# A hybrid decoder step on one NeuronCore: rows gathered three ahead, fewer of them beside the early second products, and six buffers for the spilled activations

## Chip, cores and metric

The kernel runs on one NeuronCore of one Trainium2 chip. The metric is the device time of one execution in microseconds (us), the median over runs.

## What is computed

One layer of a decoder for 512 prompt tokens and 64 sample tokens, all in float32: projections, a short convolution and a sliding-window attention, merged and normalised to `h`, and then a mixer that draws 16 experts for each of 8 heads of each token out of 16384 (128 x 128 keys):

```python
qv = jnp.einsum('nd,de->ne', xb, w_pq)                # queries
s = jnp.einsum('nhpc,hpkc->nhpk', qv, sub_keys)       # scores of the two halves of a key
top_s, top_i = lax.top_k(s, PEER_TOPK)                # 16 of each half, then 16 of their pairs
gate = jax.nn.softmax(best_s, axis=-1)
pre = jnp.einsum('nd,nhkd->nhk', xb, expert_u[idx])
coef = gate * jax.nn.gelu(pre)
out = jnp.einsum('nhk,nhkd->nd', coef, expert_v[idx])
y = _layer_norm(DEEPNORM_ALPHA * h + out, ln2_g, ln2_b)
```

## The kernel before

**Every product in three.** A weight tile of 128x1024 comes from HBM as `raw`. ScalarE rounds it to a high part `whi` and another engine subtracts to get the low part `wlo` (`split`, L118 to L120, called by `table`, L136). The TensorE takes each product as high by high, low by high and high by low (`mm3`, L122).

**Two ways to the experts.** The tokens are cut in five chunks. For three of them (`DENSE`, 384 token slots, `ND`) all 128 blocks of 128 experts are computed: a *first product* for block t (`front`, L856: the activations by `euT[t]`, 24 matmuls, then Gelu) and a *second product* (`back` and `accumulate`, L916 and L922: the Gelu values, weighted, by `ev`, 18 matmuls into six PSUM banks). Between them `middle` (L898) multiplies by the weights `gm` that say which token chose which expert, and splits the result in `chi` and `clo`. That multiplication and `clo` are VectorE's. For the other two chunks (192 columns of slots) the chosen rows alone are fetched: `experts` (L491) is a generator of 384 jobs, 192 rows of `eu` and then 192 of `ev`. GpSimd gathers a row tile `g` of 128x1024 by indirect DMA (L512), and VectorE multiplies it (`junk`, L526; `h`, L535). `GLAG = 2` rows are fetched ahead, in `GBUF = 4` buffers.

**The order of the work.** Rows are drawn by `side(n)`, which `table` calls with `pace` behind a weight's low part, on that low part's engine. In the stretch of the first products two rows and one row take turns (`PACE_U`). A weight of the scores takes none, a second product with t < NS = 60 takes one, a later one three (`PACE_V`). A scheduler puts each engine's instructions in an order when the program is built, and the engine keeps it.

**The stages.** First the projections and merges (until some 515 us). Then the scores of the dense chunks (16 weights `w_pq`), top 16 and `route` on VectorE, with 20 first products between them. Then `gate_matrix` (L774) builds one-hot tiles `hot` (`OB = 3` buffers) and writes the weights to HBM (`gd`), beside more first products. In all `AHEAD = NS + LAG = 69` first products are made by then. Those with t < 60 do not fit in SBUF: they go to HBM (`spill`) and `middle` reads them back into `re`, which has 3 buffers. Then come the *early second products*, t from 0 to 59, without first products beside them; the low part of their weight is VectorE's. `gm` is read for eight t at a time, in three DMAs. From t = 60 on each second product has a first product beside it, LAG = 9 ahead, until block 127's first product is done; the last nine second products are alone again. Then the rows end, and the three dense chunks and the rows' chunks are normalised (`finish`, L544).

Of the kernel before, what the change touches and what calls it, by code (L numbers as in the profile page):

```python
# [23 lines left out]
SEQ = 512  # L24
# [22 lines left out]
ND = 128 * len(DENSE)  # L47
# [3 lines left out]
NE = 128  # L51
NS = 60
LAG = 9
AHEAD = NS + LAG
GBUF = 4
GLAG = 2
RAW = dict(w=3, v=3)
HI = dict(w=4, v=2)
OB = 3

# [7 lines left out]
PACE_N = 18  # L68
PACE_A, PACE_B, PACE_U, PACE_V = (1, 0), (2, 1, 1), (2, 1), (1, 3)
LO_N = 50  # L70
# [5 lines left out]
def step_kernel(ctx: ExitStack, tc: tile.TileContext, I: dict, O: dict):  # L76
# [3 lines left out]
    pools = {}  # L80
# [23 lines left out]

    loads, newest = [], [None, None]

# [29 lines left out]
    def table(src, p, eng, pace=0):  # L136
        raw = tmp(p, [128, 1024], "raw", bufs=RAW[p])
        newest[0] = S.dma_start(raw, src).ins
        hi = tmp(p, [128, 1024], "whi", bufs=HI[p], dt=F32R)
        lo = tmp(p, [128, 1024], "wlo", bufs=HI[p], dt=F32R)  # L140
        last = split(hi, lo, raw, eng)
        if pace:
            with tc.issue_after(last.ins):
                side(pace)
        return hi, lo
# [16 lines left out]
    make_identity(nc, ident)  # L162
    mask_p = const("mask_p", [128, 256], src=I["mask_p"])
    convw = const("convw", [128, 4, 3], src=I["conv_w"])
# [7 lines left out]
    state = const("state", [128, 4, 8, 2], src=I["state"])  # L172
    kT_all = const("kT_all", [128, SEQ])
    v_all = const("v_all", [128, 5, 128])

# [405 lines left out]
    def weight(s, src):  # L581
        s.units += 1
        if s.w == 0:
            return table(src, "w", G if s.units % 3 != 1 else V)
        if s.units > LO_N:
            return table(src, "w", G)
        pace = PACE_A if s.units <= PACE_N else PACE_B
        if s.units % 4 == 3:
            return table(src, "w", V)
        return table(src, "w", G, pace[s.units % len(pace)])  # L590
# [219 lines left out]
    ks, bs = ExitStack(), ExitStack()  # L810
    pools["k"] = ks.enter_context(pool("k", "left"))
    pools["mm"] = ks.enter_context(psum("mm", 3))
    at_stack = ExitStack()
    pools["at"] = at_stack.enter_context(psum("at", 3))
# [26 lines left out]
    for k, tag in enumerate(("chi", "clo")):  # L841
        ln2.append(tmp("a", [128, D], tag, name=f"ln2{k}"))
        late(ln2[k], I["ln"][2 + k].broadcast_to([128, D]))
    at_stack.close()
    pools["at"] = ks.enter_context(psum("at1", 1))
# [5 lines left out]
    pools["f"] = ctx.enter_context(pool("f", "right"))  # L851
    pools["b"] = bs.enter_context(pool("b", "right"))
    hT = second.hT
# [24 lines left out]
    for k, g4 in enumerate((0, 2, 1, 3)):  # L878
        scores(second, g4)
        fronts(FQ * (k + 1))  # L880
    total = len(DENSE) * 128 // GN
    base = done
# [15 lines left out]
    def middle(t):  # L898
# [5 lines left out]
        if t < NS:  # L904
            ge = tmp("v", [128, ND], "re", bufs=3)
            S.dma_start(ge, spill[t])
        else:
            ge = coef[t]
# [7 lines left out]
    def back(t):  # L916
        co = coef.pop(t)
        wv = table(I["ev"][t * 128:(t + 1) * 128, :], "vw"[t < NS or t >= NE - LAST], V if t < NS or t > NE - 4 else G,
                   PACE_V[t >= NS])
        return co, wv  # L920

    def accumulate(ts, i, halves):  # L922
# [7 lines left out]
        return calls  # L930

    for t in range(NE + 1):
        fronts(t + LAG)
        if t < NE:
            middle(t)
        if 1 <= t <= NE - LAST:
            ops = [(t - 1, *back(t - 1))]
            for i in range(len(DENSE)):
                for args, kw in accumulate(ops, i, (0, 1)):
                    PE.matmul(*args, **kw)  # L940
# [111 lines left out]
```

## Time and profile before

| | us |
|---|---|
| median of 3 runs | 1854.08 (1852.5 to 1858.05) |
| the profiled execution | 1850.18 |
| span of its instructions | 1848.4 |
| TensorE busy with matmuls | 1723.9 (93%) |
| VectorE busy | 1464.7 (79%) |
| GpSimd busy | 1109.6 (60%) |
| ScalarE busy | 781.4 (42%) |

The span runs from the first instruction to the last, and 1.8 us lie around it. Busy shares are means over stages with different limits, so the trace is read stage by stage. In rows of the trace PE is TensorE, DVE is VectorE, ACT is ScalarE, POOL is GpSimd and SPq is the queue from which most DMAs are issued. In square brackets stands how long the engine was idle before an instruction and what ended that.

### The profile page before, as it was taken

How to read it: one execution, taken by the hardware profiler on the slowest of the kernel's cores; microseconds unless marked ns; L12 is line 12 of the kernel's file. 1: busy time of each engine (PE TensorE's matmuls, PEld its weight loads, DVE VectorE, ACT ScalarE, POOL GpSimd, SP SyncE). 2: the span in 40 equal slices, each digit the busy share in tenths (PEclk: the TensorE clock that was granted, in tenths of full speed). 3: DMA queues.
4: the chain of work that ended last, by engine and by line, in shares of the span. 5: the costliest groups of instructions: out<-in, count | busy, mean ns of one | idle time of the engine just before them, and what ended most of it. 6: DMA issues, size and time to landing. Idle time of an engine off the chain costs nothing.

```text
span 1848.4 us, 27569 instructions
## 1 busy us (share of the span) xinstructions
PE 1723.9 (93%) x9760; PEld 1566.4 (85%) x9760; DVE 1464.7 (79%) x2588; ACT 781.4 (42%) x1337; POOL 1109.6 (60%) x724
## 2 busy tenths in 40 slices
PE   7999998998799999899888899999999999999985
PEld 7998898988489899799878778778999999999974
DVE  5634579998965699987893778779788878888887
ACT  4554444443233344377794333333333333343322
POOL 4445434367857777798645422224678787778783
PEclk9999999999989999899999999999999999999998
DMA  7446443368757789899748899999999999989873
GB/s 252 134 150 225 138 132 122 115 200 300 249 201 241 235 294 311 271 349 348 289 188 303 317 333 335 336 346 339 333 314 345 337 324 350 353 307 343 314 268 104
DMA packets 190539, 496.50 MB, mean 269 GB/s; under 512 B 17712, under 2 KB 83696, under 8 KB 187312
## 3 DMA queue, kind: packets, MB, share of 16 engines
q1 hardware_dynamic: 135104, 293.39, 46.5%
q0 software_dynamic: 55296, 201.35, 30.2%
q8 instruction: 76, 1.25, 0.3%
q14 instruction: 63, 0.52, 0.1%
HBM read 454.48 MB, written 40.54 MB: 268 GB/s over the span
## 4 chain that ended last, share of the span: by engine, by line
PE 40%; DVE 23%; DMA 14%; issue 9%; POOL 8%; ACT 4%; SPq 1%; DVEq 0%; POOLq 0%; ACTq 0%
PE acc L940 15%; PE ps L123 7%; PE ps L124 7%; PE ps L125 7%; DMA g<-in_ev,idx 5%; POOL wlo L120 4%; POOL g L512 4%; DVE junk L526 3%; PE ps L796 3%; DMA re<-spill 2%; DVE wlo L120 2%; DMA raw<-in_ev 2%; DMA raw<-in_w_o 1%; ACT whi L119 1%; ACT hot L793 1%
## 5 line engine op out<-in xcount | busy, mean ns | idle before, releaser
L120 POOL TENSOR_TENSOR wlo<-raw,whi 128x1024 fp32r<-128x1024 f32 x232 | 579.1, 2499 | 301.8 <-ACT whi L119 264.7
L119 ACT ACTIVATE whi<-raw 128x1024 fp32r<-128x1024 f32 x388 | 409.5, 1056 | 603.9 <-PE ps L124 236.1
L123 PE MATMUL ps<-xhi,whi 128*128 128x384 f32 (+2 forms) x1600 | 529.9, 331 | 21.6 <-ACT sp L863 13.4
L125 PE MATMUL ps<-xhi,wlo 128*128 128x384 f32 (+2 forms) x1600 | 526.1, 329 | 3.5 <-POOL wlo L120 2.0
L124 PE MATMUL ps<-xlo,whi 128*128 128x384 f32 (+2 forms) x1600 | 526.1, 329 | 0.0
L535 DVE SCALAR_TENSOR_TENSOR h<-g,pre,h 128x1024 f32<-128x1024 f32 x192 | 309.8, 1614 | 68.3 <-DMA g<-in_ev,idx 66.8
L512 POOL DMA_INDIRECT g<-in_eu,idx x192 | 204.2, 1063 | 233.1 <-DVE junk L526 186.9
L123 PEld LDWEIGHTS ps<-xhi,whi 128*128 128x128 f32 x1600 | 308.4, 193 | 31.0 <-ACT sp L863 15.1
L512 POOL DMA_INDIRECT g<-in_ev,idx x192 | 257.0, 1338 | 124.9 <-DVE h L535 77.9
L125 PEld LDWEIGHTS ps<-xhi,wlo 128*128 128x128 f32 x1600 | 307.8, 192 | 5.3 <-POOL wlo L120 2.3
L124 PEld LDWEIGHTS ps<-xlo,whi 128*128 128x128 f32 x1600 | 308.3, 193 | 2.9 <-issue 0.3
L940 PE MATMUL acc<-whi,chi 128*128 128x512 f32 x756 | 291.4, 392 | 14.5 <-ACT chi L119 8.2
L940 PE MATMUL acc<-wlo,chi 128*128 128x512 f32 x756 | 296.9, 393 | 7.6 <-POOL wlo L120 7.6
L940 PE MATMUL acc<-whi,clo 128*128 128x512 f32 x756 | 256.4, 392 | 1.1 <-DVE clo L120 1.1
L120 DVE TENSOR_TENSOR wlo<-raw,whi 128x1024 fp32r<-128x1024 f32 x156 | 203.5, 1304 | 46.0 <-ACT whi L119 43.6
L940 PEld LDWEIGHTS acc<-whi,chi 128*128 128x128 f32 x756 | 142.6, 189 | 46.7 <-ACT chi L119 11.5
L940 PEld LDWEIGHTS acc<-wlo,chi 128*128 128x128 f32 x756 | 142.4, 188 | 38.0 <-POOL wlo L120 9.7
L526 DVE SCALAR_TENSOR_TENSOR junk<-g,hp 128x1024 bf16<-128x1024 f32 x104 | 125.9, 1210 | 56.8 <-DMA g<-in_eu,idx 54.8
L940 PEld LDWEIGHTS acc<-whi,clo 128*128 128x128 f32 x756 | 142.4, 188 | 31.3 <-DVE clo L120 1.6
L526 DVE SCALAR_TENSOR_TENSOR junk<-g,h 128x1024 bf16<-128x1024 f32 x88 | 130.9, 1488 | 3.3 <-DMA g<-in_eu,idx 3.0
L796 PE MATMUL ps<-hot 128*128 128x128 f32 x768 | 113.4, 290 | 14.5 <-ACT hot L793 13.4
L787 DVE TENSOR_TENSOR hot<-pt,T 128x1024 f32<-128x1024 f32 x96 | 113.9, 1218 | 15.8 <-PE ps L796 12.7
(250 smaller groups left out, 2157.9 us busy)
## 6 DMA issues: line engine op xcount, KB each, us to landing
raw<-in_euT SPq DMA_DIRECT2D x128, 512.0 KB
raw<-in_ev SPq DMA_DIRECT2D x128, 512.0 KB
gd<-gb SPq DMA_DIRECT2D x24, 1024.0 KB
gm<-gd SPq DMA_DIRECT2D x48, 512.0 KB
raw<-in_w_g SPq DMA_DIRECT2D x32, 512.0 KB
raw<-in_w_pq SPq DMA_DIRECT2D x32, 512.0 KB
raw<-in_w_bch SPq DMA_DIRECT2D x24, 512.0 KB
spill<-sp SPq DMA_DIRECT2D x60, 192.0 KB
```

The source lines that it names most:

```text
L119: A.activation(hi, src, AF.Copy)
L120: return (eng or V).tensor_tensor(lo, src, hi.bitcast(F32), op=ALU.subtract)
L123: PE.matmul(ps, L[0], R[0], start=start, stop=False)
L124: PE.matmul(ps, L[0], R[1], start=False, stop=False)
L125: PE.matmul(ps, L[1], R[0], start=False, stop=stop)
L512: G.indirect_dma_start(out=rows[i], out_offset=None, in_=I[src], in_offset=bass.IndirectOffsetOnAxis(ap=idx[c][:, s:s + 1], axis=0))
L526: V.scalar_tensor_tensor(junk, g, 1.0, in_psum(c), op0=ALU.mult, op1=ALU.mult, accum_out=p)
L535: V.scalar_tensor_tensor(h_tok[c], g, p, h_tok[c], op0=ALU.mult, op1=ALU.add)
L787: V.tensor_tensor(hot, iota_ps.unsqueeze(1).unsqueeze(1).broadcast_to([128, 2, 4, 128]), T[:, 0:2, n:n + 4].unsqueeze(3).broadcast_to([128 ...
L793: A.activation(oi, oi, AF.Copy, scale=weight_of)
L796: newest[1] = PE.matmul(ps[:, r * 128:(r + 1) * 128], hot[:, 1, r, :], oi, start=True, stop=True).ins
L940: PE.matmul(*args, **kw)
```

## The change

Nothing of the arithmetic changes. The edits:

- `GLAG` 2 to 3 and `GBUF` 4 to 5: rows are fetched three ahead, in five buffers.
- A weight of the dense chunks' scores now draws one row (`PACE_Q = 1`). Of three early second products two draw a row, where each did.
- `NS` 60 to 63 and `LAG` 9 to 6: AHEAD stays 69. Three more blocks are spilled and read back, three fewer are kept.
- `re` has 6 buffers, `hot` has 4.
- For t up to 63, what `middle(t)` puts on VectorE is ordered behind the low part of the weight of the second product two back (`last_lo`, in fact that of t - 2).
- To make room, the mask, `kT_all` and `v_all` of the attention lie in a pool that is closed after it, and the pool `b` is opened anew before the gates.

```diff
@@ -49,14 +49,14 @@
 NG = ND // GN
 IB = 8
 NE = 128
-NS = 60
-LAG = 9
+NS = 63
+LAG = 6
 AHEAD = NS + LAG
-GBUF = 4
-GLAG = 2
+GBUF = 5
+GLAG = 3
 RAW = dict(w=3, v=3)
 HI = dict(w=4, v=2)
-OB = 3
+OB = 4
 
 
 ORDER = "qkscscasacsca"
@@ -66,7 +66,7 @@
 
 
 PACE_N = 18
-PACE_A, PACE_B, PACE_U, PACE_V = (1, 0), (2, 1, 1), (2, 1), (1, 3)
+PACE_A, PACE_B, PACE_Q, PACE_U, PACE_V = (1, 0), (2, 1, 1), 1, (2, 1), (1, 3)
 LO_N = 50
 GATED = "aaag"
 OUT = "aaav"
@@ -102,7 +102,7 @@
     def tmp(p, shape, tag, name=None, bufs=1, dt=F32):
         return pools[p].tile(shape, dt, tag=tag, name=name or tag, bufs=bufs)
 
-    loads, newest = [], [None, None]
+    loads, newest = [], [None, None, None]
 
     def late(dst, src):
 
@@ -139,6 +139,7 @@
         hi = tmp(p, [128, 1024], "whi", bufs=HI[p], dt=F32R)
         lo = tmp(p, [128, 1024], "wlo", bufs=HI[p], dt=F32R)
         last = split(hi, lo, raw, eng)
+        newest[2] = last.ins
         if pace:
             with tc.issue_after(last.ins):
                 side(pace)
@@ -160,7 +161,6 @@
 
     ident = const("ident", [128, 128])
     make_identity(nc, ident)
-    mask_p = const("mask_p", [128, 256], src=I["mask_p"])
     convw = const("convw", [128, 4, 3], src=I["conv_w"])
     sink_p = const("sink_p", [128, 8], src=I["sink_p"])
     sink_s = const("sink_s", [128, 2, 2], src=I["sink_s"])
@@ -170,8 +170,6 @@
     ucar = const("ucar", [128, 4, 2])
     V.memset(ucar, 0.0)
     state = const("state", [128, 4, 8, 2], src=I["state"])
-    kT_all = const("kT_all", [128, SEQ])
-    v_all = const("v_all", [128, 5, 128])
 
     iota128 = const("iota128", [128, 128], src=I["iota128"])
     h_tok, idx, gate = {3: const("h3", [128, D])}, {}, {}
@@ -583,7 +581,7 @@
         if s.w == 0:
             return table(src, "w", G if s.units % 3 != 1 else V)
         if s.units > LO_N:
-            return table(src, "w", G)
+            return table(src, "w", G, PACE_Q)
         pace = PACE_A if s.units <= PACE_N else PACE_B
         if s.units % 4 == 3:
             return table(src, "w", V)
@@ -810,6 +808,11 @@
     ks, bs = ExitStack(), ExitStack()
     pools["k"] = ks.enter_context(pool("k", "left"))
     pools["mm"] = ks.enter_context(psum("mm", 3))
+    kvs = ExitStack()
+    pools["kv"] = kvs.enter_context(pool("kv", "right"))
+    mask_p, kT_all = tmp("kv", [128, 256], "mask_p"), tmp("kv", [128, SEQ], "kT_all")
+    v_all = tmp("kv", [128, 5, 128], "v_all")
+    loads.insert(0, (mask_p, I["mask_p"]))
     at_stack = ExitStack()
     pools["at"] = at_stack.enter_context(psum("at", 3))
     sel3 = ([tmp("k", [128, 128], f"k3{k}") for k in range(2)], tmp("k", [128, 128], "gt3"))
@@ -841,6 +844,7 @@
     for k, tag in enumerate(("chi", "clo")):
         ln2.append(tmp("a", [128, D], tag, name=f"ln2{k}"))
         late(ln2[k], I["ln"][2 + k].broadcast_to([128, D]))
+    kvs.close()
     at_stack.close()
     pools["at"] = ks.enter_context(psum("at1", 1))
     shared = [pools["at"].tile([128, 512], F32, tag="at", name="pt")]
@@ -849,7 +853,7 @@
     scratch.append(shared[0])
     pools["hp"] = ks.enter_context(psum("hp", 1))
     pools["f"] = ctx.enter_context(pool("f", "right"))
-    pools["b"] = bs.enter_context(pool("b", "right"))
+    pools["b"] = bs.enter_context(pool("b0", "right"))
     hT = second.hT
     coef = {}
 
@@ -878,6 +882,8 @@
     for k, g4 in enumerate((0, 2, 1, 3)):
         scores(second, g4)
         fronts(FQ * (k + 1))
+    bs.close()
+    pools["b"] = bs.enter_context(pool("b", "right"))
     total = len(DENSE) * 128 // GN
     base = done
     for i in range(len(DENSE)):
@@ -902,7 +908,7 @@
                 S.dma_start(gm[0][:, g:g + NG // 3].rearrange("p g i n -> p g (i n)"),
                             gd[g:g + NG // 3, :, t:t + IB, :].rearrange("g p i n -> p g (i n)"))
         if t < NS:
-            ge = tmp("v", [128, ND], "re", bufs=3)
+            ge = tmp("v", [128, ND], "re", bufs=6)
             S.dma_start(ge, spill[t])
         else:
             ge = coef[t]
@@ -916,7 +922,7 @@
     def back(t):
         co = coef.pop(t)
         wv = table(I["ev"][t * 128:(t + 1) * 128, :], "vw"[t < NS or t >= NE - LAST], V if t < NS or t > NE - 4 else G,
-                   PACE_V[t >= NS])
+                   PACE_V[1] if t >= NS else PACE_V[0] * (t % 3 > 0))
         return co, wv
 
     def accumulate(ts, i, halves):
@@ -929,12 +935,18 @@
                                   dict(start=(t == 0 and p == 0), stop=(t == NE - 1 and p == 2))))
         return calls
 
+    last_lo = None
     for t in range(NE + 1):
         fronts(t + LAG)
-        if t < NE:
+        if last_lo is not None and t <= NS:
+
+            with tc.issue_after(last_lo):
+                middle(t)
+        elif t < NE:
             middle(t)
         if 1 <= t <= NE - LAST:
             ops = [(t - 1, *back(t - 1))]
+            last_lo = newest[2] if t <= NS else None
             for i in range(len(DENSE)):
                 for args, kw in accumulate(ops, i, (0, 1)):
                     PE.matmul(*args, **kw)
```

Three places of the order. **GpSimd, in the dense chunks' scores** (`wlo<-raw,whi` is a weight's low part, `g<-in_eu` the gather of a row; before):

```order
L512 DMA g<-in_eu,idx_95 128x1024 x2
L120 TENSOR_TENSOR wlo<-raw,whi 128x1024 x5
L512 DMA g<-in_eu,idx_95 128x1024 x2
L120 TENSOR_TENSOR wlo<-raw,whi 128x1024
L512 DMA g<-in_eu,idx_95 128x1024
L120 TENSOR_TENSOR wlo<-raw,whi 128x1024
```

and with the change:

```order
L510 DMA g<-in_eu,idx_92 128x1024
L120 TENSOR_TENSOR wlo<-raw,whi 128x1024
L510 DMA g<-in_eu,idx_92 128x1024
L120 TENSOR_TENSOR wlo<-raw,whi 128x1024
L510 DMA g<-in_eu,idx_92 128x1024
L120 TENSOR_TENSOR wlo<-raw,whi 128x1024 x2
L510 DMA g<-in_eu,idx_92 128x1024 x2
```

The runs of five low parts, the score weights, have rows between them now.

**VectorE, where the second products begin** (`re<-re,gm` is the weighting in `middle`, `junk` a row; before):

```order
L910 TENSOR_TENSOR re<-re,gm 128x384 x2
L120 TENSOR_TENSOR clo<-re,chi 128x384 x2
L526 SCALAR_TENSOR_TENSOR junk,pre<-g,hp 128x1024
L910 TENSOR_TENSOR re<-re,gm 128x384
L526 SCALAR_TENSOR_TENSOR junk,pre<-g,hp 128x1024 x2
L910 TENSOR_TENSOR re<-re,gm 128x384 x2
L526 SCALAR_TENSOR_TENSOR junk,pre<-g,hp 128x1024
L120 TENSOR_TENSOR wlo<-raw,whi 128x1024
L526 SCALAR_TENSOR_TENSOR junk,pre<-g,hp 128x1024
L120 TENSOR_TENSOR wlo<-raw,whi 128x1024
```

and with the change:

```order
L916 TENSOR_TENSOR re<-re,gm 128x384 x2
L120 TENSOR_TENSOR clo<-re,chi 128x384 x2
L524 SCALAR_TENSOR_TENSOR junk,pre<-g,hp 128x1024 x4
L120 TENSOR_TENSOR wlo<-raw,whi 128x1024
L916 TENSOR_TENSOR re<-re,gm 128x384
L524 SCALAR_TENSOR_TENSOR junk,pre<-g,hp 128x1024 x2
L120 TENSOR_TENSOR wlo<-raw,whi 128x1024
L916 TENSOR_TENSOR re<-re,gm 128x384
```

Five weightings stood before the first low part, two do now.

**GpSimd, at the end** (the low parts of the last second products and the last gathers; before):

```order
L120 TENSOR_TENSOR wlo<-raw,whi 128x1024
L512 DMA g<-in_ev,idx_98 128x1024 x3
L120 TENSOR_TENSOR wlo<-raw,whi 128x1024
L512 DMA g<-in_ev,idx_98 128x1024
L120 TENSOR_TENSOR wlo<-raw,whi 128x1024
L512 DMA g<-in_ev,idx_98 128x1024 x3
L120 TENSOR_TENSOR wlo<-raw,whi 128x1024 x2
```

and with the change:

```order
L120 TENSOR_TENSOR wlo<-raw,whi 128x1024
L510 DMA g<-in_ev,idx_95 128x1024 x3
L120 TENSOR_TENSOR wlo<-raw,whi 128x1024
L510 DMA g<-in_ev,idx_95 128x1024 x3
L120 TENSOR_TENSOR wlo<-raw,whi 128x1024
L510 DMA g<-in_ev,idx_95 128x1024 x5
```

The last two low parts stood behind all gathers; now five gathers stand behind the last low part.

## Rows read from the trace of the kernel before

**Rows 1.** Busy time by stretch; columns as in the second line.

```profile
core 0 of [0], span 1848.4 us
core 0: us, PE busy (x) PEld busy (x) DVE busy (x) ACT busy (x) POOL busy (x), PEclk, DMA share, GB/s
516.00:640.00 124.00, 123.05 (x747) 118.18 (x745) 68.14 (x299) 46.11 (x68) 84.14 (x49) 0.99 0.70 235
640.00:780.00 140.00, 125.10 (x701) 122.55 (x702) 139.62 (x424) 56.41 (x78) 107.05 (x67) 0.95 0.83 283
780.00:901.00 121.00, 121.00 (x814) 120.80 (x813) 100.00 (x123) 86.91 (x209) 104.86 (x97) 0.99 0.95 346
901.00:978.00 77.00, 62.55 (x413) 55.31 (x412) 71.29 (x74) 68.36 (x198) 35.03 (x54) 0.96 0.52 209
978.00:1033.00 55.00, 45.12 (x247) 44.34 (x245) 22.23 (x23) 18.07 (x25) 30.30 (x18) 0.93 0.89 303
1033.00:1296.00 263.00, 254.46 (x1106) 208.61 (x1107) 210.36 (x313) 91.52 (x122) 74.90 (x66) 0.99 0.98 338
1296.00:1781.00 485.00, 485.00 (x2451) 441.28 (x2450) 412.65 (x353) 172.84 (x237) 375.08 (x229) 1.00 0.92 329
```

**Rows 2.** Chain that ended last: second products; start us, us, what.

```profile
1249.89 24.79 PE acc L940 x108
...
1470.16 4.12 PE acc L940 x18
...
1478.47 4.12 PE acc L940 x18
```

**Rows 3.** Waits of PE, 1033 to 1296 us: total, times, longest.

```profile
PE acc L940 <- ACT chi L119: 8.2, 8, 1.6
PE acc L940 <- ACT whi L119: 5.3, 1, 5.3
```

**Rows 4.** DMA, 1033 to 1296 us: all packets; the rows' queue (packets, MB, share).

```profile
DMA packets 50800, 88.94 MB, mean 338 GB/s; under 512 B 3244, under 2 KB 34834, under 8 KB 50782
...
q0 software_dynamic: 9293, 33.87, 34.9%
```

**Rows 5.** Timeline near 1140 us, by engine: start us, us, instruction, [idle before].

```profile
1129.84 4.94 SPq L902 DMA_DIRECT2D gm<-gd  x3
...
1137.90 0.85 SPq L906 DMA_DIRECT2D re<-spill  x2
...
1146.00 0.56 DVE L910 TENSOR_TENSOR re<-re,gm 128x384 f32<-128x384 f32 x1 [4.42 <-DMA re<-spill]
...
1147.22 0.50 PE L940 MATMUL acc<-whi,chi 128*128 128x512 f32 x1 [0.98 <-ACT chi L119]
```

**Rows 6.** Timeline, 1010 to 1034 us, PE and DVE.

```profile
1012.80 0.69 PE L123 MATMUL ps<-xhi,whi 128*128 128x384 f32 x1 [4.85 <-ACT gel L867]
...
1014.40 4.58 DVE L910 TENSOR_TENSOR re<-re,gm 128x384 f32<-128x384 f32 x2 [10.17 <-DMA re<-spill]
...
1021.16 3.42 DVE L120 TENSOR_TENSOR wlo<-raw,whi 128x1024 fp32r<-128x1024 f32 x1 [1.04 <-ACT whi L119]
```

**Rows 7.** Groups of DVE, 640 to 780 us: xcount | busy us, mean ns | idle before.

```profile
L526 DVE SCALAR_TENSOR_TENSOR junk<-g,hp 128x1024 bf16<-128x1024 f32 x35 | 42.1, 1203 | 0.0
```

**Rows 8.** Waits: DVE from 516 to 640 us, then PE from 640 to 783 us.

```profile
DVE junk L526 <- DMA g<-in_eu,idx: 52.8, 10, 14.3
...
PE ps L123 <- ACT sp L863: 12.9, 3, 6.3
```

**Rows 9.** Timeline of the end, DVE and POOL.

```profile
1771.77 1.22 DVE L120 TENSOR_TENSOR wlo<-raw,whi 128x1024 fp32r<-128x1024 f32 x1
...
1807.09 1.36 POOL L512 DMA_INDIRECT g<-in_ev,idx  x1 [0.30 <-issue]
...
1810.13 6.77 DVE L535 SCALAR_TENSOR_TENSOR h<-g,pre,h 128x1024 f32<-128x1024 f32 x3 [2.02 <-DMA g<-in_ev,idx]
```

**Rows 10.** Waits of PE, 1781 to 1831 us.

```profile
PE acc L940 <- POOL wlo L120: 7.6, 5, 2.9
```

## The prediction

> **What bounds the kernel now.** I read the busy times by stretch first, since a mean over the span hides that the limits change [rows 1]. From 516 to 640 us TensorE is busy for 123.05 of 124 us. From 640 to 780 us VectorE is: 139.62 of 140 us, while TensorE has 15 us of holes. From 780 to 901 us TensorE is full again. From 901 to 978 us the gates run almost alone, VectorE at 71.29 of 77 us. From 978 to 1033 us, where the last ten first products run and the second products are to begin, no engine is full and the DMA share is 0.89. From 1033 to 1296 us, the early second products, TensorE has 254.46 of 263 us and the DMA engines stand at 0.98. From 1296 to 1781 us TensorE is busy all the time, and nothing that the change does to other engines can show there.
>
> Next, what a product costs when nothing waits. Six second products follow each other in 24.79 us, 4.1 us each, and where a first product stands between two of them they are 8.3 us apart (1478.47 less 1470.16), so a first product costs 4.2 us [rows 2]. Now the losses can be read. In the early second products 60 x 4.1 + 4.2 (the 1106 matmuls are 60 x 18 and one first product) is 250 of 263 us: 13 us lost. From 978 to 1033 us ten first products are 42 of 55 us: again 13 us lost.
>
> Then the waits say why. TensorE waits for `chi` eight times there [rows 3], and the timeline shows one of them from its beginning: three reads of `gm` occupy the queue from 1129.84 us, the reads of `re` go out behind them at 1137.90 us, VectorE sits idle 4.42 us for one, and at 1147.22 us TensorE has its hole [rows 5]. The hole is counted 0.98 us, but the whole step is longer. It comes with each block of eight. The DMA engines have no slack to catch up: 88.94 MB in 263 us is the 338 GB/s of that stretch [rows 4].
>
> **The change part by part.** I set each term against the profiled execution, 1850.2 us (its span of 1848.4 and 1.8 around it).
>
> *Early second products.* Each now draws 2/3 of a row. 33.87 MB went to 66 rows, 0.51 MB each [rows 4]. With 44 rows instead, and three more blocks at (88.94 - 33.87) / 60 = 0.92 MB, the stretch moves 88.94 - 11.3 + 2.8 = 80.4 MB, which takes 238 us at the same rate, while TensorE needs 63 x 4.1 + 4.2 = 262 us. The DMA engines stop being the limit. Six buffers let a read of `re` go out five blocks ahead of its use, so it stands before the `gm` reads and not behind them, and a weighting that still waits has the low part of an older weight before it, not behind. Of the 13 us I take 11 as won. Bounds: 13, all of it, and 0, if `gm` itself is late.
>
> *Start of the second products.* VectorE waits 10.17 us for the fourth `re`, which has no buffer until the first is used up; a low part that TensorE needs comes only behind it, at 1021.16 us [rows 6]. In the new order two weightings precede the first low part, where five did, and the buffers suffice for six reads. ScalarE's wait for weights, which gave TensorE the hole of 4.85 us at 1012.80 us, is the DMA's, and remains in part. Of the 13 us lost I take 6, bounds 10 and 0.
>
> *Scores and routes.* By the two orders 92 rows stood before the first `hot` on VectorE and 112 do now. Eleven of the twenty more stand before the last burst of top-16 work. There VectorE is idle, 52.8 us of it in waits for rows that were fetched too late [rows 8]; rows three ahead shorten these, so I cost them at nothing. If that cover fails they cost what the next ones cost. The other nine stand in the burst and among the routes (36 rows between the first candidates and the last key, now 43). From 640 to 780 us VectorE has no idle time, and a row is 1.20 us [rows 7], 1.28 us with the read of its sum (42.1 us for 35 rows, and the small instruction after each, an estimate). Nine are 11.5 us. GpSimd has room for them (107.05 of 140 us). The waits of TensorE there, 12.9 us, are for Gelus that stand on ScalarE behind an exponential that waits for VectorE [rows 8]; so TensorE waits longer when VectorE is later. One wait of VectorE for a row inside the burst goes with rows three ahead; I take +9 us. Bounds: 0, and 20 x 1.28 = 25.6 us. One first product moves from behind this stretch to before it, which costs nothing in the sum.
>
> *Gates.* A fourth `hot` buffer cannot help where VectorE is full, but TensorE has 14.5 us of holes from 901 to 978 us: I take 2 us, bounds 4 and 0.
>
> *Three second products moved, and the end.* They cost 12.3 us more among the early ones, and 12.3 us less at the end, but the end is not TensorE's alone. Its anchor is VectorE's last low part for a first product, at 1771.77 us. From there 15 rows end at 1816.90 us [rows 9], 45.1 us later, and the span ends 76.6 us later. TensorE waits 7.6 us for low parts that GpSimd makes between gathers [rows 10]. Now 17 rows follow that anchor, with three fewer of GpSimd's low parts in between, since three fewer products are left. The rows will take about as long as before, 38 to 50 us, and they, not TensorE, lead. Behind the last of them stood 31.5 us of products and normalising. In the new order the last products' VectorE work stands ahead of the last rows, so 8 to 12 us of that run beside them. I take 66 us from the anchor to the end (60 to 74), 10.6 less than 76.6. With the 12.3 us this is +1.7, bounds -4 and +10.
>
> *The first 516 us.* By the order, attention and convolution work of the first 100 us changes places on TensorE, and there is a buffer for one more load. I take 0, bounds -3 and +3.
>
> Sum: -11 - 6 + 9 - 2 + 1.7 = -8.3, so 1841.9 us. The median of the runs stands 3.9 above the profiled execution, so 1845.8, rounded to **1846 us**. Of the second products from 1296 us on nothing is counted: 59 pairs before, 59 now.
>
> **The rivals.** *The waits stay (no change).* What ends the waits at each block could be `gm` itself, 1.5 MB in short pieces, which no new buffer brings earlier, and the six buffers then do not do what they are for: reads of `re` are placed one for each weight, as before. For it: the `gm` reads take 4.94 us of the queue. Against it: VectorE's wait names `re` [rows 5]. Then the 11 us stay lost: -8.3 + 11 = +2.7, 1856.8 us.
>
> *The routes pay for it (slower).* If the rows that I put into idle time arrive there no earlier, VectorE takes all 20 in its full stretch, and the keys, on which all gates wait, come 25.6 us later instead of 9. It decides from the point where the top-16 burst near 620 us begins later than now. For it: VectorE is full from 640 us on, and rows were late before. Against it: 56 us of VectorE are free before that. -8.3 + 16.6 = +8.3, 1862.4 us.
>
> *Rows hold up the weights (slower).* Eleven rows more and two in the burst before 640 us are 6.7 MB, 19.3 us of DMA at the 346 GB/s of the next stretch but one; if all of it delayed weights, the sum would be +11.0, 1865.1 us. Against it: the share there is 0.70, so 37 of 124 us are free [rows 1]. This is a rule of the Trainium skill, in "DMA: Bandwidth & Descriptors", section on queues, rings and completion order: each DMA engine takes its queues in turn, so a gather is not behind the weights but between them. [...]
>
> **How the numbers follow.** What a measurement of this kernel can tell from no change is about 0.3%, 5.6 us. My forecast, faster, has 0.52; its own range is 1831 to 1849 (routes at nothing, the start at 10 and the waits at 13 give -23). The waits stay has 0.27 and is within 0.3%. The routes have 0.17 and the weights 0.04; both are slower. So faster 0.52, same 0.27, slower 0.21. The range for 8 in 10 goes from 1831 to the routes' 1862; beyond lie the weights' case and the far ends of the end term.
>
> **What would show it.** In the changed profile: the DMA share of the early second products below 0.95 and 63 of them in under 268 us; TensorE's waits for `chi` there below 3 us; the first second product within 50 us of the last gate; VectorE full from some 630 us until the keys, and that stretch some 9 us longer than now; the rows' end about 45 us behind the last first product's low part. I am wrong if the waits for `chi` stay at 8 us, if the keys come 15 us or more later, or if the end, counted from that low part, is not shorter than 74 us.

## The result, and the profile after

The change makes the kernel faster: 1829.55 us, the median of 4 runs (1827.41 to 1834.04), beside 1855.26 for the kernel before (1852.5 to 1858.05). The ratio is 0.9871, with a 95% interval of 0.9845 to 0.9897. The direction was forecast, the size was not: 1846 us had been predicted, and the result lies 1.5 us below the low end of the range. The profiled execution of the changed kernel was the slowest of its four, 1834.04 us, and that of the kernel before was faster than all its timed runs, so the two traces differ by 16.4 us of span where the medians differ by 25.7. Stages can only be told of those 16.4 us.

Busy time by stretch of the kernel before, cut where the work changes: to the last transpose after the first normalisation, scores and routes to the gates' first transpose, gates to their last matmul, start of the second products, early second products, pairs (a second product and a first product in turn), and from the first lone second product to the end:

```profile
core 0: us, PE busy (x) PEld busy (x) DVE busy (x) ACT busy (x) POOL busy (x), PEclk, DMA share, GB/s
0.00:516.54 516.54, 468.17 (x3128) 425.59 (x3128) 387.25 (x922) 223.43 (x379) 264.00 (x127) 0.95 0.55 183
516.54:778.08 261.54, 245.70 (x1436) 238.51 (x1436) 205.66 (x720) 101.21 (x142) 189.29 (x115) 0.97 0.77 261
778.08:978.73 200.65, 186.20 (x1239) 178.75 (x1240) 173.21 (x198) 156.73 (x407) 141.79 (x152) 0.97 0.78 291
978.73:1033.31 54.58, 44.39 (x242) 43.65 (x240) 22.54 (x25) 17.60 (x24) 30.34 (x18) 0.92 0.90 306
1033.31:1295.56 262.25, 254.01 (x1104) 208.19 (x1105) 209.61 (x311) 91.08 (x121) 74.86 (x65) 0.99 0.98 338
1295.56:1781.47 485.91, 485.91 (x2456) 442.04 (x2455) 413.09 (x354) 173.28 (x238) 375.55 (x229) 1.00 0.92 329
1781.47:1848.40 66.93, 39.55 (x163) 29.67 (x161) 53.38 (x63) 18.01 (x27) 33.72 (x20) 0.89 0.45 151
```

The same seven stretches of the changed kernel:

```profile
0.00:522.13 522.13, 471.93 (x3128) 428.25 (x3128) 388.37 (x922) 222.99 (x379) 273.16 (x130) 0.95 0.54 184
522.13:793.53 271.40, 253.52 (x1466) 243.83 (x1465) 221.91 (x760) 102.83 (x144) 211.22 (x135) 0.97 0.85 291
793.53:982.27 188.74, 179.10 (x1210) 171.86 (x1211) 166.09 (x192) 154.30 (x405) 133.39 (x146) 0.98 0.78 292
982.27:1031.78 49.51, 43.77 (x241) 42.84 (x240) 12.63 (x19) 14.99 (x22) 29.45 (x18) 0.97 0.96 339
1031.78:1294.45 262.67, 261.91 (x1158) 216.96 (x1159) 199.68 (x288) 97.83 (x130) 48.70 (x47) 1.00 0.94 318
1294.45:1780.36 485.91, 485.91 (x2456) 442.06 (x2455) 444.47 (x357) 172.90 (x237) 374.77 (x232) 1.00 0.93 329
1780.36:1832.00 51.64, 25.40 (x109) 19.93 (x107) 43.13 (x57) 13.46 (x21) 21.73 (x15) 0.79 0.44 146
```

Stage by stage the trace after stands at +5.6, +9.9, -11.9, -5.1, +0.4, 0.0 and -15.3 us. The fifth row has three products more than before and takes the same time: TensorE is busy for 261.91 of 262.67 us, where it had 254.01 of 262.25. Below, the *loss* of that stretch is its length less 4.08 us for each second product and 4.2 for the one first product that lies in it. 4.08 is how far the steps of the changed kernel lie apart when nothing waits (weightings start at 1236.44 and 1240.52 us). The loss was 13.3 us and is 1.5.

The waits in that stretch of the changed kernel (total, times, longest) answer to [rows 3]:

```profile
PE acc L952 <- ACT gel L871: 1.1, 1, 1.1
DVE re L916 <- DMA re<-spill: 0.7, 1, 0.7
PE acc L952 <- ACT whi L119: 0.6, 1, 0.6
PE acc L952 <- DVE clo L120: 0.2, 1, 0.2
```

No wait for `chi` is left, of 8.2 us. VectorE's waits for `re` in the kernel before, in the same view, were these:

```profile
DVE re L910 <- DMA re<-spill: 27.2, 10, 4.4
```

The end, on the timeline of the changed kernel; the two rows answer to [rows 9]: the last low part for a first product, and the last row.

```profile
1763.57 1.22 DVE L120 TENSOR_TENSOR wlo<-raw,whi 128x1024 fp32r<-128x1024 f32 x1
...
1804.48 1.28 DVE L533 SCALAR_TENSOR_TENSOR h<-g,pre,h 128x1024 f32<-128x1024 f32 x1
```

From that low part 17 rows end 42.2 us later, and the span 68.4 us later (76.6 before).

### The profile page after: what moved, and what is told of

Read it like the earlier page. It is cut to its first block, busy times and chain, and to the rows that moved or that the text cites. A ratio compares the mean times of both kernels' runs of the same rounds, so it can differ in the third digit from the quotient of the medians.

```text
span 1832.0 us, 27597 instructions
## 1 busy us (share of the span) xinstructions
PE 1721.6 (94%) x9760; PEld 1565.7 (85%) x9760; DVE 1476.3 (81%) x2591; ACT 779.3 (43%) x1337; POOL 1092.4 (60%) x721
## 5 line engine op out<-in xcount | busy, mean ns | idle before, releaser
L533 DVE SCALAR_TENSOR_TENSOR h<-g,pre,h 128x1024 f32<-128x1024 f32 x192 | 294.7, 1535 | 40.0 <-DMA g<-in_ev,idx 38.0
L952 PE MATMUL acc<-wlo,chi 128*128 128x512 f32 x756 | 291.1, 391 | 1.6 <-POOL wlo L120 1.6
L510 POOL DMA_INDIRECT g<-in_ev,idx x192 | 240.7, 1253 | 86.1 <-issue 34.9
L952 PE MATMUL acc<-whi,chi 128*128 128x512 f32 x756 | 281.1, 389 | 1.7 <-ACT gel L871 1.1
L952 PE MATMUL acc<-whi,clo 128*128 128x512 f32 x756 | 272.0, 391 | 0.2 <-DVE clo L120 0.2
L120 DVE TENSOR_TENSOR wlo<-raw,whi 128x1024 fp32r<-128x1024 f32 x159 | 207.5, 1305 | 75.9 <-ACT whi L119 75.7
L524 DVE SCALAR_TENSOR_TENSOR junk<-g,hp 128x1024 bf16<-128x1024 f32 x120 | 145.4, 1211 | 50.4 <-DMA g<-in_eu,idx 48.4
L794 PEld LDWEIGHTS ps<-hot 128*128 128x128 f32 x768 | 103.9, 195 | 16.6 <-ACT hot L791 14.2
```

What stands on the lines that cost most here:

```text
L120: return (eng or V).tensor_tensor(lo, src, hi.bitcast(F32), op=ALU.subtract)
L510: G.indirect_dma_start(out=rows[i], out_offset=None, in_=I[src], in_offset=bass.IndirectOffsetOnAxis(ap=idx[c][:, s:s + 1], axis=0))
L524: V.scalar_tensor_tensor(junk, g, 1.0, in_psum(c), op0=ALU.mult, op1=ALU.mult, accum_out=p)
L533: V.scalar_tensor_tensor(h_tok[c], g, p, h_tok[c], op0=ALU.mult, op1=ALU.add)
L794: newest[1] = PE.matmul(ps[:, r * 128:(r + 1) * 128], hot[:, 1, r, :], oi, start=True, stop=True).ins
```

## The experiments

Three chips were used, with four kernels on each, and the kernel before was timed on every one: 1853.61, 1850.94 and 1856.44 us, medians of 15, 21 and 17 runs. Its single runs spread from 1843 to 1864 us, so totals are compared by ratios, and reasons by stages.

### Which part removes the waits of the early second products

Three parts act there: fewer rows (two of three products draw one), six `re` buffers, and the weighting queued behind a low part. First each was undone alone, together with the lead of the rows.

**A row for every product again.**

```diff
-PACE_A, PACE_B, PACE_Q, PACE_U, PACE_V = (1, 0), (2, 1, 1), 1, (2, 1), (1, 3)
+PACE_A, PACE_B, PACE_Q, PACE_U, PACE_V = (1, 0), (2, 1, 1), 0, (2, 1), (1, 3)
-                   PACE_V[1] if t >= NS else PACE_V[0] * (t % 3 > 0))
+                   PACE_V[1] if t >= NS else PACE_V[0])
```

> The change, but each early second product draws a row again and the score weights none. Theory supply (the 11.8 us that the early second products lose less come from the rows that were taken out, since the DMA engines stood at 0.98 of their time): the loss there is 8 us or more again at a DMA share of 0.97 or more, while scores and routes take some 265 us instead of 271. Theory buffers (they come from the six buffers for the spilled activations): the loss stays under 4 us, and the kernel is no slower than the changed one.

1829.23 us, ratio 0.9864 (0.983 to 0.9898). The stretch of the early second products, and what TensorE waits for in it:

```profile
1017.52:1287.50 269.98, 260.74 (x1136) 212.41 (x1137) 217.19 (x318) 94.47 (x127) 73.66 (x66) 1.00 0.97 333
PE acc L952 <- ACT whi L119: 10.7, 8, 3.2
```

The first product that lies in this stretch elsewhere stands behind it here: TensorE has 63 x 18 matmuls and two, and the pairs are 489.8 us long instead of 485.9. So only 0.3 us go off for first products, and the loss is 12.6 us, at a DMA share of 0.97. Fewer rows thus win 11.1 us in the stage, as the theory of supply had it. The waits are for weights, not for `re`, and from the second on they stand 33 to 36 us apart, one for each block of eight, 14 to 18 us behind its reads of `gm`. Whether the rows delay the weights by their traffic or by VectorE's time (217.2 us busy, 199.7 in the changed kernel) was not tried apart. The median is no higher for it all the same. Behind the first 516 us the profile is 3.0 us longer: scores, routes and gates take 5.5 us less, and the end 3.4 us less (48.2), since rows drawn in one stage need not be drawn in another.

**Three `re` buffers again.**

```diff
-            ge = tmp("v", [128, ND], "re", bufs=6)
+            ge = tmp("v", [128, ND], "re", bufs=3)
```

> The change with three buffers for the spilled activations instead of six. Theory buffers: the early second products lose 8 us or more again, and the start before them is 4 us or more longer. Theory supply: they lose under 4 us with three buffers too, and the time is within 3 us of the changed kernel's.

1840.63 us, ratio 0.9921 (0.9888 to 0.9954). The loss is 16.5 us, more than before the change, though the DMA share is only 0.89; the start stays short (50.8 us).

```profile
DVE re L916 <- DMA re<-spill: 61.8, 28, 7.4
PE acc L952 <- DVE clo L120: 10.2, 6, 2.9
```

The longest of these waits, on the timeline of VectorE and of SP's queue: two reads of `gm`, then the read of `re`, which takes 5.19 us to issue, and a weighting that waits 7.42 us.

```profile
1210.74 1.00 SPq L908 DMA_DIRECT2D gm<-gd  x2
1211.85 5.19 SPq L912 DMA_DIRECT2D re<-spill  x1
...
1222.49 0.56 DVE L916 TENSOR_TENSOR re<-re,gm 128x384 f32<-128x384 f32 x1 [7.42 <-DMA re<-spill]
```

In the changed kernel the queue stops at the same place, for 3.52 us, and no weighting waits:

```profile
1241.10 1.00 SPq L908 DMA_DIRECT2D gm<-gd  x2
1242.19 3.52 SPq L912 DMA_DIRECT2D re<-spill  x1
...
1248.68 0.56 DVE L916 TENSOR_TENSOR re<-re,gm 128x384 f32<-128x384 f32 x1
```

**The weighting not queued behind a low part.**

```diff
-        if last_lo is not None and t <= NS:
+        if last_lo is not None and t < 0:
```

> The change without the order that puts VectorE's weighting behind the low part two products back. Theory order (a weighting that waits for its read held up low parts): the early second products lose 5 us or more, and the start is longer. Theories supply and buffers: no difference of more than 3 us.

1846.9 us, ratio 0.995 (0.9928 to 0.9972). The loss is 25.1 us, at a DMA share of 0.87: without this one line the other parts are worse than none.

```profile
DVE re L916 <- DMA re<-spill: 64.2, 31, 6.7
PE acc L952 <- DVE clo L120: 12.6, 10, 3.8
```

The longest wait for `clo` (VectorE, then TensorE): the weighting waits for its read (the next one then 1.2 us for `gm`), `clo` of an older block stands behind them on VectorE, and TensorE waits for that `clo`.

```profile
1219.03 0.56 DVE L916 TENSOR_TENSOR re<-re,gm 128x384 f32<-128x384 f32 x1 [6.67 <-DMA re<-spill]
...
1221.90 0.79 PE L952 MATMUL acc<-whi,clo 128*128 128x512 f32 x1 [3.85 <-DVE clo L120]
```

VectorE waits for `re` as with three buffers, though it has six. Set against its product, a weighting starts 14 to 28 us ahead (from the ninth product on, first matmul of the k-th product less start of the k-th weighting; 7 to 18 in the changed kernel), and when it starts only one to three reads have been issued that no earlier weighting took, its own among them: the buffers hold weighted blocks that wait for their product.

These results called for each part alone, so three more kernels have two of the three undone.

**Only the fewer rows** (edits of the second and third experiment).

> Of the three parts for the early second products (fewer rows, six re buffers, weighting queued behind a low part) only the fewer rows: three buffers, and the weighting where the scheduler puts it; all else as changed. Theory 'the parts work only together' (six buffers hold reads ahead only if the weightings are held back; without that VectorE weights each read as it lands and waits for the next): VectorE's wait for re 60 us or more, loss of the early second products 16 to 26 us at a DMA share under 0.90, time 1838 to 1848. Rival 'the parts add': fewer rows win by themselves the 7.3 us that they win beside the others (8.8 less 1.5), so the loss is about 6 us, the wait for re under 20 us and the time about 1834.

1844.15 us, ratio 0.993 (0.9909 to 0.9951). Loss 13.7 us at a share of 0.90, a little below the 16 that was expected; the wait for `re` is 54.5 us and not 60. The parts do not add: 6 us was the rival's number. (The 7.3 and 8.8 us in the expectation took off a first product that does not lie in that stretch; with 11.1 the rival's number is about 2.)

```profile
DVE re L916 <- DMA re<-spill: 54.5, 26, 7.2
PE acc L952 <- DVE clo L120: 9.2, 6, 4.4
```

**Only the six buffers** (edits of the first and third).

> Only the six re buffers: a row for every product, and the weighting where the scheduler puts it. Theory 'the parts work only together': the weightings run 15 us or more ahead of their products, reads of re stand no more than 3 ahead, VectorE waits 25 us or more for re, and the loss is 13 to 25 us, no less than the 13 us of the kernel before; time 1838 to 1850. Rival 'the parts add': the buffers win the 15 us by themselves, the loss is under 3 us and the time about 1826.

1846.49 us, ratio 0.9957 (0.9931 to 0.9982). No first product lies in the stretch here (275.55 us with 63 x 18 matmuls), so the loss is 18.5 us. That is within what was expected, but the reason is not the expected one: VectorE has no wait for `re` to speak of. What is late is the weights, once by 5.4 us and seven times by less.

```profile
PE acc L952 <- ACT whi L119: 12.2, 8, 5.4
```

**Only the order** (edits of the first and second).

> Only the weighting queued behind the low part: a row for every product, three re buffers. Theory 'the parts work only together': reads of re at most 3 ahead as in the kernel before, VectorE's wait for re 20 us or more, loss 10 to 18 us; time 1834 to 1842. Rival 'the parts add': the order alone wins what its removal cost, more than all 13 us; the loss is under 3 us and the time about 1826.

1835.61 us, ratio 0.9899 (0.9859 to 0.994). No first product lies in the stretch here either (266.20 us), so the loss is 9.2 us, a little below the 10 to 18 of the first theory and far from the rival's 3. Its profiled execution is its fastest, 1825.77 us, and the others are 1835 to 1842, so these 9.2 may be at the low edge. The DMA engines are fuller here than in any other of these kernels, 0.99 and 343 GB/s:

```profile
DVE re L916 <- DMA re<-spill: 36.4, 7, 6.7
PE acc L952 <- ACT chi L119: 4.6, 5, 2.9
PE acc L952 <- ACT whi L119: 0.8, 1, 0.8
```

The eight combinations, with how long before its weighting a block is read (start of the k-th L912, L906 before, to start of the k-th weighting; median from the eleventh on):

| rows fewer | six buffers | order | loss, us | DMA share | read ahead, us | VectorE waits for re |
|---|---|---|---|---|---|---|
| | | | 13.3 | 0.98 | 8.0 | 27.2 |
| x | | | 13.7 | 0.90 | 5.7 | 54.5 |
| | x | | 18.5 | 0.95 | 9.5 | 0.1 |
| | | x | 9.2 | 0.99 | 6.4 | 36.4 |
| x | x | | 25.1 | 0.87 | 5.9 | 64.2 |
| x | | x | 16.5 | 0.89 | 5.9 | 61.8 |
| | x | x | 12.6 | 0.97 | 19.4 | 0.0 |
| x | x | x | 1.5 | 0.94 | 10.7 | 0.7 |

The first line is the kernel before, which differs in other stages too; with the division of the products changed in it (below) its loss is 13.0. Kernels with all three parts and a change elsewhere gave 1.7, 1.9, 2.6 and 3.3. So differences of 5 us and more can be read from one profile, smaller ones not. What follows: where the median read goes out 9.5 us ahead or more, VectorE does not wait for `re` to speak of; where it goes out 8.0 us ahead or less, it does. (At 6 us the column says no more than the last one: a read lands 6.2 us after it is issued, median in this stretch of the changed kernel, and a weighting that waits starts when its read lands.) Buffers alone bring the reads forward, and then the weights are late; fewer rows alone do not, and in three of four pairs they bring no gain (13.3 to 13.7, 18.5 to 25.1, 9.2 to 16.5). Only beside both other parts do they gain, 12.6 to 1.5. The same holds for the buffers (13.3 to 18.5, 13.7 to 25.1, 9.2 to 12.6, but 16.5 to 1.5). The order alone gains 4.1 us there, less than one profile can tell, but its total is 9 to 11 us below those of the other two single parts, timed on the same chip. Why six buffers without the order leave no wait for `re` where the rows are many was not tried further.

### What shortens the end

**Rows two ahead again, four row buffers.**

```diff
-GBUF = 5
-GLAG = 3
+GBUF = 4
+GLAG = 2
```

> The change with rows two ahead in four buffers, as before. Theory lead (the end, 15.3 us shorter though three products of 12.2 us left it, owes some of that to rows that are fetched earlier): from the last pair of products to the end it takes 58 us or more, not 51.6. Theory fewer (the end is shorter because three products with their low parts on GpSimd left it): it stays under 55 us. In scores and routes VectorE's waits for rows grow in either case, and that stretch is up to 5 us longer.

1825.93 us, ratio 0.9837 (0.9795 to 0.9878): not slower. Its pairs and its end, by stretch, are 2.4 and 6.3 us longer than in the changed kernel:

```profile
1278.63:1766.98 488.35, 486.42 (x2455) 441.92 (x2455) 447.89 (x353) 172.84 (x237) 380.80 (x229) 1.00 0.92 325
1766.98:1824.94 57.96, 26.32 (x109) 19.76 (x107) 48.56 (x62) 13.46 (x21) 28.34 (x19) 0.79 0.48 158
```

So the lead wins in the stage of the end what was expected of it. Ahead of that the stages are shorter in this profile, 264.2 us of scores and routes and 183.2 of gates, and a gain of the lead in the total is not shown.

**60 and nine products instead of 63 and six** (`re` with four buffers, for room).

```diff
-NS = 63
-LAG = 6
+NS = 60
+LAG = 9
```

> The changed kernel with the products divided as before: 60 early second products and nine first products left at the end, instead of 63 and six (four re buffers, for room). Theory 'fewer products left shorten the end': from the first lone second product to the end 60 us or more instead of 51.6, while the early second products, three fewer, are 12.3 us shorter, and the last nine lone products 12.3 us longer; so against the sum of the changed kernel the end loses 3 us or less by the division alone, and the time is 1829 to 1836. Rival 'the end gains from the lead of the rows alone': the tail is what the three products add, 12.3 us, so 64 us, and the time does not move beyond 3 us. If the start of the second products is shortened by the division and not by the buffers, the stretch from the last gate to the first of them goes from 49.5 back to 54 us.

1841.16 us, ratio 0.9962 (0.9936 to 0.9988). The end is 63.8 us, the rival's 64: 12.2 us longer than 51.6, which is what three products more take. The total is longer because four buffers are no better than three: the loss is 16.0 us, with 39.6 us of waits for `re`. Pairs and end less those three products are 485.9 + 63.8 - 12.2 = 537.5 us, as in the changed kernel.

**The kernel before with 63 and six**, all else as before.

```diff
-NS = 60
-LAG = 9
+NS = 63
+LAG = 6
```

> The kernel before with nothing changed but the division of the products: 63 early second products and six first products left. Theory 'the division alone brings the shorter start': from the last gate to the first second product about 50 us instead of 54.6; the loss of the early second products stays at 13 us or more, since rows, buffers and order are as before; from the first lone second product to the end about 58 us, as with rows two ahead. Then the time is 1848 to 1854. Rival 'the division is worth nothing by itself': start 54 us, end 62 us or more, time 1853 to 1857.

1848.69 us, ratio 0.9975 (0.9948 to 1.0002). The end is 52.6 us, below both numbers, but the pairs are longer:

```profile
1300.65:1790.15 489.50, 486.43 (x2455) 441.90 (x2455) 443.88 (x353) 172.96 (x237) 375.28 (x229) 1.00 0.93 327
1790.15:1842.73 52.58, 28.21 (x109) 20.91 (x107) 42.36 (x57) 13.46 (x21) 21.60 (x14) 0.80 0.39 127
```

Pairs and end are 542.1 us; in the kernel before they are 552.8, less 12.2 for the three products 540.6. The division alone is worth nothing there. The start is 55.6 us, so it isn't the division that shortened it.

**Rows two ahead until the pairs, three from there.**

```diff
+        def ahead(n):
+            while len(begun) < min(n, len(jobs)):
+                fetch(len(begun))
+                begun.append(1)
...
-        for i in range(GLAG):
-            fetch(i)
+        ahead(lead[0])
...
-            if i + GLAG < len(jobs):
-                fetch(i + GLAG)
+            ahead(i + 1 + lead[0])
...
+        if t == NS:
+            lead[0] = GLAG
```

> The changed kernel with rows two ahead until the first of the pairs and three ahead from there (five row buffers throughout). If the lead costs time ahead of the gates and brings it at the end, this has the scores and routes of two ahead (264 us instead of 271) and the end of three ahead (52 us instead of 58), and runs in 1819 to 1824. Rival 'the lead costs nothing ahead of the gates, and the difference there is between runs': scores and routes 267 to 271 us and the time 1825 to 1830.

1826.27 us, ratio 0.9855 (0.9812 to 0.9899). Pairs and end are as with three ahead, 485.9 and 51.8 us, so it is there that the lead counts. Scores and routes are 270.2 us, as the rival had it. But the last kernel below does the same work there, also two ahead, and takes 264.8: this stage differs by 5 us between profiles, and whether the lead costs anything ahead of the gates can't be read from one.

What can be read is the start of the second products. This kernel differs from the changed one in the lead alone, and its start is 53.0 us instead of 49.5. The difference is TensorE's wait right before its first second product; before the change, here, and in the changed kernel:

```profile
1033.31 0.77 PE L940 MATMUL acc<-whi,chi 128*128 128x512 f32 x1 [5.34 <-ACT whi L119]
1024.34 0.77 PE L959 MATMUL acc<-whi,chi 128*128 128x512 f32 x1 [4.54 <-ACT whi L120]
1031.78 0.47 PE L952 MATMUL acc<-whi,chi 128*128 128x512 f32 x1 [1.07 <-ACT gel L871]
```

All five kernels with rows two ahead there have this wait, 3.7 to 5.3 us, with or without the other parts; in the nine with three ahead it is 1.7 us or less.

### What shortens the gates

**Three `hot` buffers again.**

```diff
-OB = 4
+OB = 3
```

> The changed kernel with three hot buffers again, all else as changed. Theory 'the fourth buffer shortens the gates': the stretch from the gates' first transposes to their last matmul goes from 188.7 back to 196 to 201 us, TensorE's wait for ScalarE's hot from 5.1 back to 10 us or more, and the time is 6 to 12 us above the changed kernel's 1829.6, so 1836 to 1842. Rival 'the shorter gates come from the order in which first products and gates interleave': the stretch stays at 183 to 191 us, the wait for hot below 8 us, and the time within 4 us of 1829.6.

1836.63 us, ratio 0.99 (0.9868 to 0.9932). The gates take 194.2 us, between the two theories; in the five kernels above with four buffers, rows three ahead and the same matmuls there they take 187.5 to 188.7. TensorE's waits for ScalarE's scaled copies:

```profile
PE ps L794 <- ACT hot L791: 11.2, 18, 2.3
```

In the kernel before, and what VectorE waited for at the same time:

```profile
PE ps L796 <- ACT hot L793: 13.4, 22, 2.4
DVE hot L787 <- PE ps L796: 12.7, 17, 2.2
```

In the changed kernel:

```profile
PE ps L794 <- ACT hot L791: 5.1, 11, 1.6
DVE hot L785 <- PE ps L794: 9.3, 8, 2.0
```

The fourth buffer thus brings 5.5 us of the 11.9. Another 5.0 us are no gain: 29 matmuls of first products (x1239 before, x1210 now, 4.2 us for 24) have moved to the stage ahead. Some 1.4 us remain unexplained.

**A fifth `hot` buffer**, on the kernel with two and then three ahead.

```diff
-OB = 4
+OB = 5
```

> The kernel with rows two ahead until the pairs and three from there, with a fifth hot buffer. Theory 'the wait for hot is the want of a buffer': it went from 11.2 us with three buffers to 5.1 with four, and goes to under 2 us with five; the gates take 181 to 185 us and the time is 1820 to 1825. Rival 'ScalarE itself is the limit by then': the wait for hot stays at 4 us or more, the gates at 185 us or more and the time at 1825 to 1829.

1828.32 us, ratio 0.9847 (0.9801 to 0.9894). The wait for `hot` is 3.9 us and TensorE waits 4.9 us for the copies of finished gates instead; the stage is 183.4 us where its base had 185.2. Neither a stage nor the total shows a gain beyond what runs differ by. No kernel of this study is faster than the changed one by more than its interval.

## Why the prediction was right in sign and a third of the size

| term | predicted, us | traces, us |
|---|---|---|
| first 516 us | 0 (-3 to +3) | +5.6 |
| scores and routes | +9 (0 to 25.6) | +9.9 |
| gates | -2 (-4 to 0) | -11.9 |
| start | -6 (-10 to 0) | -5.1 |
| early second products | -11 (-13 to 0) | -11.8 (0.4 less 3 x 4.08) |
| pairs | 0 | 0.0 |
| three products moved, and the end | +1.7 (-4 to +10) | -3.1 (12.2 - 15.3) |
| sum | -8.3 | -16.4 |

The traces hold 16.4 of the 25.7 us. The rest is no stage's: the profiled execution before lies 5.1 us below its median and the one after 4.5 us above, where the prediction took 3.9 us for both.

**Early second products: right in size, and incomplete in the reason.** The signs that were named came: a DMA share of 0.94, 63 products in 262.7 us, no wait for `chi`. All three parts are needed: undoing the rows costs 11.1 us, the buffers 15.0, the order 23.6. "The DMA engines stop being the limit", which rested on [rows 4], holds as one condition. The three kernels with the change that draw a row for every product move 89.9 to 91.4 MB in the stretch, and none loses less than 9.2 us; the one at the highest rate, 343 GB/s, takes 266.2 us for 91.4 MB, where 63 products need 257. (The changed kernel moves 83.6 MB, not 80.4, since 25.7 MB of rows still fall into the stretch.) But it was told as if it were enough, and with a share of 0.87 to 0.90 and without the buffers, the order or both, 13.7 to 25.1 us are lost. What the order does was sized right and described wrongly: a weighting that waits was to hold up "the low part of an older weight", and for that TensorE waits 0.7 us at most in any of the eight. It waits for `clo`, and the order's worth is that the six buffers hold reads and not weighted blocks. The rival that the waits stay falls with VectorE's wait for `re`, from 27.2 to 0.7 us.

**Gates: the step that failed most.** It said that "a fourth `hot` buffer cannot help where VectorE is full", from the last 77 us of the stage. Over all of it VectorE was busy for 173 of 201 us, and 12.7 us of its idle time were waits for TensorE to give back a `hot` buffer, while TensorE waited 13.4 us for `hot`. Waits on both sides of a ring were a reason to try a buffer, and undoing it is worth 5.5 us in the stage. They are no proof that the next one helps: with four both sides still wait (5.1 and 9.3 us), and a fifth brought no gain that shows. With the 5.0 us of the moved matmuls taken out of two terms, gates are -6.9 and scores and routes +4.8.

**Scores and routes: the size was right and the reason is doubtful.** Twenty more rows on VectorE were to cost 9 us. But three kernels that draw three more rows there, not twenty (94 against 91 products with `junk` until the gates, 111 in the changed kernel), took 267.0, 270.6 and 266.7 us without the moved matmuls, where the kernel before took 261.5 and, with its products divided otherwise, 261.3. So the +4.8 is there without the rows. In the three, TensorE waits 21.2 to 22.0 us for ScalarE's Gelu, against 13.4 both before and after. What lengthens this stage stays open: three kernels with rows two ahead and the twenty rows took 264.2, 270.2 and 264.8 us, and the pools were not tried apart. The rival that routes pay for it needed 25.6 us and is out.

**The end: the anchor moved.** From the last low part of a first product the end was forecast at 66 us (it is 68.4), with rows 45 us behind it (42.2). What failed is that the anchor itself was taken to come no sooner: it now stands 16.8 us ahead of the end of the pairs (1763.57 and 1780.36), where it stood 9.7 us ahead. The lead of the rows in the pairs does most of that: with two ahead it stands 11.2 us ahead, and pairs and end take 546.3 us, with three 537.5.

**Start: right size, another reason.** It was put down to the buffers and the order, and it is short without the buffers (50.8 us), without the order (49.9), and with a row for every product (50.3); the division alone does not shorten it (55.6). The runs show the lead of the rows in its place, which this term did not name: with two ahead the start is 52.6 to 55.6 us in five kernels, with three ahead 47.8 to 50.8 in eight and 52.6 in one, which has 60 and nine products and waits elsewhere. What in the order of the work the lead changes there was not tried further.

**The first 516 us: the bound was too narrow.** The kernel before and its version with another division issue the same work on TensorE there, and took 516.5 and 508.7 us; nine kernels with the change and the same order on TensorE took 512.6 to 522.8. So +5.6 us says nothing of the change, and +/-3 should have been 8.

**Rows and weights.** "Rows hold up the weights" was given 4 in 100. Against it stood the free DMA time, and beside it the rule of the Trainium skill, in "DMA: Bandwidth & Descriptors", section on queues, rings and completion order, that an engine takes its queues in turn. The page has these turns packet by packet; how the engines' time is shared it does not say, and in [rows 4] the rows' queue had 34.9% of it. No such delay shows before the gates. In the early second products, with the other parts in place, a row for every product leaves TensorE waiting 10.7 us for weights, two of three 0.6 us; with the buffers alone it is 12.2 us, with the order alone 0.8. So rows did hold up weights, in a stage where the prediction did not look for it. Whether the turns of the queues are the reason, no run here shows.

## What to carry to other kernels

More buffers for a read can fill with finished work when its consumer runs ahead, and then the engine waits for each read as it did before: with fewer rows, six buffers left 64.2 us of waits for `re` without the order and 0.7 with it. When a stage has several knobs on one chain, cost them together: here two of the three parts were worth nothing or less alone, and one line of order was worth 24 us beside the others. Before a ring is called no bottleneck, read the waits on both of its sides over the whole stage. And before the same stretch of two kernels is compared, count what lies in it: one product that crosses the border was worth 4.2 us here.

## What the runs showed of the hardware that was not expected

A DMA share near 1 does not say how large the loss is: 0.99 at 343 GB/s went with 9.2 us, 0.87 at 289 GB/s with 25.1. And the same program moves by more than single terms of a prediction: runs of the kernel before spread from 1843 to 1864 us, and the same work of TensorE ahead of the first normalisation's end differed by 7.8 us between two profiles.
